# A bidirectional mLSTM and delta-rule encoder block on one core: one store of the inverses per half of the rows, another model behind the instruction order, and weight splits 60 places higher

## The chip, the cores and the metric

The kernel runs on one core of a Trainium2 chip. A core has five engines with a queue each: TensorE (PE, matrix products), VectorE (DVE), ScalarE (ACT), GpSimd (POOL) and SyncE (SP). Each takes its own instructions strictly in the order in which they stand in its queue, and the engines wait for each other through semaphores. Transfers are issued from the queues of SP, ACT and POOL. The metric is the device time of one execution, in microseconds; several executions are timed, and their median is given.

## The reference

One layer of an encoder for 256 tokens of width 2048, in float32. Cut to what matters here:

```python
mod = silu(c) @ W_ada + b_ada                 # six vectors: shift, scale, gate, twice
h = rms_norm(x) * (1 + scale_m) + shift_m
proj = h @ w_in                               # q,k,v,gates of mLSTM | q,k,v,z of GDN | merge gates
h_a = bidirectional(mlstm_chunkwise, ...)     # 4 heads of 256 x 512
o_b = bidirectional(gated_delta_chunkwise, ...)   # 16 heads of 128 x 128
x = x + gate_m * ((g_a * (h_a @ w_branch_a) + g_b * (o_b @ w_branch_b)) @ w_out)
hf = rms_norm(x) * (1 + scale_f) + shift_f
gt, up = split(hf @ w_gate_up)
x = x + gate_f * ((silu(gt) * up) @ w_down)
return rms_norm(x)
```

The delta rule (GDN) inverts a unit lower triangular matrix for each head and direction:

```python
a_mat = eye + beta * (k @ k.T) * decay_strict
t_mat = triangular_solve(a_mat, eye, lower=True, unit_diagonal=True)
u = t_mat @ (beta * v);  w = t_mat @ (beta * exp(g) * k)
```

## The kernel before

**Weights in two parts.** Every large product is run with weights and activations split in a high part (a cast to the fast float32 format) and a low part (the rest). A weight block of 1 MB is loaded to a buffer `raw` from SP's queue; ACT casts half of it to `wh` and DVE subtracts to get `wl` (128 x 1024 each); then PE multiplies high by high, high by low and low by high. `fjob` (from line 148) does so for a block of 128 output columns, products 256 wide; `tjob` (from line 169) for 512 columns, products 512 wide, two accumulators. Splits are lines 157 and 158 in `fjob`, 182 and 183 in `halves` of `tjob`. `raw`, `wh` and `wl` have three buffers each. A job is a generator; each step yields after half a block.

**Stages.** (1) The two adaLN vectors that the first norm needs are summed by DVE while the first 16 column blocks are multiplied. (2) Gates, convolutions and phase 1 of the first four delta-rule heads. (3) For each of four groups of four heads: `gdn_invert`, `gdn_blocks` and two passes of `gdn_phase2` (two heads each, some nine steps), while the next heads' projections (`b_job`, `fjob`) and the list `fills` (projections of z, of mLSTM and of the merge gates) give PE other work; the remaining adaLN sums run in the background on DVE, through the same `raw` buffers. (4) mLSTM beside the branch projections, then the output projection. (5) The feed-forward part: gate and up in 11 column groups, then down, and the final norm.

**The inverses.** Phase 1 of head h (from line 537) cuts the 32 x 32 diagonal blocks of its matrices, for two directions and two halves of the tokens, and moves them through DRAM (`inst_d`) so that each of the 16 blocks of a head is one partition of the tile `uu` (64 partitions, 32 x 32 each, for the four heads of a group): line 607, head `hl_` of the group to partitions 16 `hl_` to 16 `hl_` + 15. `gdn_invert` (from line 619) inverts all 64 blocks at once by back substitution on DVE, 30 pairs of instructions pinned in order. Rows 16 to 31 are final when i is 16, rows 0 to 15 at the end, and each half is stored by `store` (line 627): one transfer for each of the four heads, on POOL's queue, because `inv_d` holds the heads innermost. `gdn_blocks` (from line 650) loads the inverses from `inv_d` with four transfers, also POOL's, to a tile `cg`, transposes it on DVE (line 656), mixes it to `R` (lines 660 and 661) and copies it to `X` and `UL`. Phase 2 begins with products by `R` (line 689).

**What sets the order.** The program is traced in the order of the Python code, and each instruction gets its place in the trace as its priority. A scheduler then runs a model of the machine: whenever an engine of the model is free, it takes, of the instructions whose inputs and buffers are ready in the model, the one with the lowest place. What comes out is a fixed list for each engine. An instruction passed through `order` is pinned behind the one traced before it on its engine. So the list depends on how long the model thinks that instructions and transfers take; on the chip nothing is reordered any more, and an instruction that is not ready holds up all that stand behind it in its queue.

Of the kernel before, what the change touches and what calls it, by code (L numbers as in the profile page):

```python
# [9 lines left out]
F32 = mybir.dt.float32  # L10
F32R = mybir.dt.float32r
AF = mybir.ActivationFunctionType
ALU = mybir.AluOpType
# [8 lines left out]
NH_B, DK_B = 16, 128  # L22
# [2 lines left out]
KD = 11  # L25
GRP = 4
N0 = 4 + 3 * GRP


PK_ADAB = 0  # L30
# [22 lines left out]
def hybrid_block(ctx: ExitStack, tc: tile.TileContext, xr, nfr, crow, pk_d, cst_d, ada2, ada4, win0, winb, wint, wba, wbb, wo, wgu, wd, out, dbg=None):  # L53
    nc = tc.nc
    V, S, G, PE = nc.vector, nc.scalar, nc.gpsimd, nc.tensor
# [29 lines left out]
    def order(ins, yes=True):  # L85

        return tc.keep_in_program_order(ins) if yes else ins
# [60 lines left out]
    def fjob(name, src, done):  # L148

        ps = acc_ps.tile([P, 512], F32, tag="acc", name=f"acc_{name}")  # L150
        o = ps[:, :T]
        raw = st.tile([P, KB, P], F32, tag="raw", bufs=3, name=f"raw_{name}")
        nc.sync.dma_start(raw, src)
        for k0 in range(0, KB, 8):
            wh = st.tile([P, 8, P], F32R, tag="wh", bufs=3, name=f"wh_{name}_{k0}")
            wl = st.tile([P, 8, P], F32R, tag="wl", bufs=3, name=f"wl_{name}_{k0}")
            S.activation(wh, raw[:, k0 : k0 + 8], AF.Copy)  # L157
            V.tensor_tensor(wl, raw[:, k0 : k0 + 8], wh.bitcast(F32), ALU.subtract)  # L158
            for k in range(8):
                for i, x in enumerate((hh, hl)):  # L160
                    PE.matmul(o, wh[:, k], both(x, k0 + k).rearrange("p a b -> p b a"), start=k0 + k + i == 0, stop=False)  # L161
            for k in range(8):
                PE.matmul(o, wl[:, k], both(hh, k0 + k).rearrange("p a b -> p b a"), start=False, stop=k0 + k == KB - 1)
            if k0:
                pump()
                done(o.rearrange("p (b a) -> p a b", a=2))
            yield True

    def tjob(name, chunks, xh, xl, done, early=0, by_token=None, steps=1):

        raws = {}

        def halves(u, k0):
            if u not in raws:
                raws[u] = st.tile([P, 4, 512], F32, tag="raw", bufs=3, name=f"raw_{name}_{u}")
                nc.sync.dma_start(raws[u], chunks[u])
            wh = st.tile([P, 2, 512], F32R, tag="wh", bufs=3, name=f"wh_{name}_{u}_{k0}")  # L180
            wl = st.tile([P, 2, 512], F32R, tag="wl", bufs=3, name=f"wl_{name}_{u}_{k0}")
            order(S.activation(wh, raws[u][:, k0 : k0 + 2], AF.Copy), early)  # L182
            order(V.tensor_tensor(wl, raws[u][:, k0 : k0 + 2], wh.bitcast(F32), ALU.subtract), early)  # L183
            return wh, wl

        todo = [(u, k0) for u in range(len(chunks)) for k0 in (0, 2)]
        made = []
        for i, q in enumerate(todo[:early]):
            made.append(halves(*q))
            if steps > 1 or i == early - 1:  # L190
                yield True
        ps = [acc_ps.tile([P, 512], F32, tag="acc", name=f"acc_{name}_{t}") for t in range(2)]
        last = 4 * len(chunks) - 1
        if by_token:
            todo = todo[:-2]
        for n, (u, k0) in enumerate(todo):
            wh, wl = made.pop(0) if made else halves(u, k0)
            kt = [(4 * u + k0 + k, k, t) for k in range(2) for t in range(2)]
            for kk, k, t in kt:
                order(PE.matmul(ps[t], tok(xh, kk, t), turns(wh[:, k]), start=kk == 0, stop=False), early and steps > 1)  # L200
                PE.matmul(ps[t], tok(xl, kk, t), turns(wh[:, k]), start=False, stop=False)  # L201
            for kk, k, t in kt:
                PE.matmul(ps[t], tok(xh, kk, t), turns(wl[:, k]), start=False, stop=kk == last)  # L203
            if k0:
                pump()
                if u == len(chunks) - 1:
                    done(ps)
            yield True
            if early and steps > 1:
                if n + early < len(todo):  # L210
                    made.append(halves(*todo[n + early]))
                yield True
        if by_token:
            w = [halves(len(chunks) - 1, k0) for k0 in (0, 2)]
            by_token()
            for t in range(2):
                for k in range(4):
                    kk = last - 3 + k
                    wh = turns(w[k // 2][0][:, k % 2])
                    PE.matmul(ps[t], tok(xh, kk, t), wh, start=False, stop=False)  # L220
                    PE.matmul(ps[t], tok(xl, kk, t), wh, start=False, stop=False)
                for k in range(4):
                    kk = last - 3 + k
                    PE.matmul(ps[t], tok(xh, kk, t), turns(w[k // 2][1][:, k % 2]), start=False, stop=kk == last)
                done(t, ps[t])
                yield True
# [29 lines left out]
    mb_d = [tc.dram_tile([P, 2, 512], F32, name=f"mb_d{g}") for g in range(4)]  # L256
    ob_d = [tc.dram_tile([4, P, T], F32, name=f"ob_d{g}") for g in range(4)]
    inst_d = [tc.dram_tile([64, 32, 32], F32, name=f"inst_d{g}") for g in range(NH_B // GRP)]
    inv_d = [tc.dram_tile([32, 4, 16, 32], F32, name=f"inv_d{g}") for g in range(NH_B // GRP)]

    hh, hl = (bigA.tile([P, KB // 2, 2, 2, P], F32R, tag="b16", name=n) for n in ("hh", "hl"))

# [179 lines left out]
    with ExitStack() as s0:  # L442
        w0 = pool(s0, "w0")

        x = w0.tile([P, KB, T], F32, name="x")
        ss = w0.tile([P, 2], F32, name="ssx")
        rows = w0.tile([P, T], F32, name="rows")
# [13 lines left out]
        def loads(b):  # L461
            ra = [w0.tile([P, D + 2], F32, tag="ra", bufs=5, name=f"ra{b}_{i}") for i in range(2)]
            raw = st.tile([P, N0, P], F32, tag="raw", bufs=3, name=f"raw0_{b}")
            for i in range(2):
# [13 lines left out]
        ra, raw = loads(0)  # L478
# [18 lines left out]
        for b in range(KB):  # L497
            if b:
                ra, raw = loads(b)
# [35 lines left out]
    uus = {}  # L535

    def gdn_phase1(h):
# [61 lines left out]
        g, hl_ = divmod(h, GRP)  # L599
        if g not in uus:  # L600
            uus[g] = bk.tile([64, 32, 32], F32, tag="uu", bufs=1, name=f"uu{g}")
        inst = inst_d[g][16 * hl_ : 16 * hl_ + 16]
        for b in range(4):
            G.dma_start(
                inst[4 * b : 4 * b + 4].rearrange("x j i -> j x i"), mi[32 * b : 32 * b + 32, :, 32 * b : 32 * b + 32]
            )
        G.dma_start(uus[g][16 * hl_ : 16 * hl_ + 16], inst)

        cc = ccs[h % NB]
        for b in range(4):  # L610
# [8 lines left out]
    def gdn_invert(g):  # L619

        uu = uus.pop(g)
        tmp = bk.tile([64, 256], F32, tag="utmp", bufs=1, name=f"utmp{g}")
        inv = inv_d[g].rearrange("j b (x h) i -> h (b x) j i", h=GRP)

        def store(rows):
            for e in range(GRP):
                G.dma_start(inv[e, :, rows], uu[16 * e : 16 * e + 16, rows])

        yield
        order(V.memset(uu.rearrange("p j i -> p (j i)")[:, ::33], 1.0))  # L630
        size = 0
        for i in range(30, 0, -1):
            w = 31 - i
            t3 = tmp[:, 0 : i * w].rearrange("p (j c) -> p j c", j=i)
            order(V.tensor_tensor(
                t3,
                uu[:, 0:i, i : i + 1].broadcast_to([64, i, w]),
                uu[:, i : i + 1, i + 1 :].broadcast_to([64, i, w]),
                ALU.mult,
            ))  # L640
            order(V.tensor_tensor(uu[:, 0:i, i + 1 :], uu[:, 0:i, i + 1 :], t3, ALU.add))
            if i == 16:
                store(slice(16, 32))
            size += i * w + 125
            if size > 720:
                size = 0
                yield
        store(slice(0, 16))

    def gdn_blocks(g):  # L650

        cg = bk.tile([P, 2, 512], F32, tag="uu", bufs=1, name=f"cg{g}")
        for b in range(4):
            G.dma_start(cg[32 * b : 32 * b + 32, 0], inv_d[g][:, b].rearrange("j x i -> j (x i)"))
        yield
        order(V.transpose(cg[:, 1], cg[:, 0]))
        F_, Bt, Ft, B_ = (cg[:, i // 2, (i % 2) * 256 : (i % 2 + 1) * 256].rearrange("p (m c) -> p m c", m=8) for i in range(4))

        def mix(dst, a, ca, b, cb):
            order(V.tensor_scalar(dst, b, cb, None, ALU.mult))  # L660
            order(V.scalar_tensor_tensor(dst, a, ca, dst, ALU.mult, ALU.add))

        mix(R[:, 0], Ft, even, Bt, odd)
        mix(R[:, 1], B_, even, F_, odd)
        yield
        for i, ab in enumerate(((Ft, Bt), (B_, F_))):
            for b in range(4):
                r = slice(32 * b, 32 * b + 32)
                order(S.activation(X[r, i, :, b % 2], ab[b // 2][r], AF.Copy))
            yield  # L670
        for i, a in enumerate((F_, B_)):
            for b in range(4):
                r = slice(32 * b, 32 * b + 32)
                order(S.activation(UL[r, i, :, r], a[r], AF.Copy))
            yield
# [535 lines left out]
    for j in range(FB // 4):  # L1211
# [4 lines left out]
        for e2 in range(2):  # L1216
            px = gps(f"pxf{j}_{e2}")
            for e in range(2):
                f = 2 * e2 + e
                for t in range(2):  # L1220
                    PE.transpose(px[:, e * T + t * P : e * T + (t + 1) * P], sg[:, t, f * P : (f + 1) * P], ident)
            b = 4 * j + 2 * e2
# [143 lines left out]
```

## Time and profile before

| | |
|---|---|
| median of 3 runs | 2038.97 us (2037.25 to 2042.45) |
| the profiled execution | 2036.88 us, its span 2035.0 us |
| TensorE busy | 1956.7 us, 96% |
| VectorE, ScalarE, GpSimd busy | 1394.1, 1050.0 and 106.4 us |
| mean granted TensorE clock | 0.987 |
| DMA | 485.64 MB, 239 GB/s over the span |

The profile is one execution. Rows of groups give busy time, the mean duration in ns, the idle time of the engine ahead of the instruction and what ended it. PEld is TensorE's loading of weights, which overlaps its products. The granted clock is the share of full speed that TensorE was given. Times within the span count from its start. A wait is idle time of an engine, put down to what ended it.

### The profile page before, as it was taken

Reading aid. Unit: us, or ns where it says so; the run is one execution under the profiler, and the core shown is the slowest. Engines: PE = TensorE matmul, PEld = TensorE weight load, DVE = VectorE, ACT = ScalarE, POOL = GpSimd, SP = SyncE. Lnnn points to the kernel's source line nnn. Section 1 sums busy time; section 2 is a strip of 40 time slices with the busy share of each in tenths; the row PEclk is TensorE's granted clock in tenths of the full one; section 3 lists DMA queues with packets and bytes.
Section 4 is the critical chain, followed back from the end, with each engine's and each line's share of the span. In section 5 each row is a group of like instructions: output and inputs, shape, how many; then the busy total and the mean of one; then the engine's idle time right before and its main releaser. Section 6 shows DMA issues by size and latency. Waiting matters only on the chain.

```text
span 2035.0 us, 27065 instructions
## 1 busy us (share of the span) xinstructions
PE 1956.7 (96%) x10374; PEld 1706.4 (84%) x10374; DVE 1394.1 (69%) x2059; ACT 1050.0 (52%) x1582; POOL 106.4 (5%) x205
## 2 busy tenths in 40 slices
PE   8999999999999899999899999999999999999997
PEld 6777879988888788988878788778888888888886
DVE  5778777777889588855677679866666665555554
ACT  3147547755775577565444444554444444444443
POOL 0002210010101010100200000000000000000000
PEclk9999999999999899999999999999999999999999
DMA  9986664556766465766987669656767666566563
GB/s 399 420 325 222 178 215 153 190 171 220 241 230 197 178 211 212 243 238 240 360 297 264 212 245 390 256 186 249 252 244 262 235 246 212 204 206 204 199 200 142
DMA packets 78962, 485.64 MB, mean 239 GB/s; under 512 B 10585, under 2 KB 15969, under 8 KB 24433
## 3 DMA queue, kind: packets, MB, share of 16 engines
q1 hardware_dynamic: 63360, 450.95, 61.2%
q0 software_dynamic: 8160, 17.88, 3.8%
q10 hardware_dynamic: 7314, 15.10, 2.0%
q8 instruction: 81, 1.33, 0.3%
q14 instruction: 47, 0.39, 0.1%
HBM read 467.07 MB, written 16.82 MB: 238 GB/s over the span
## 4 chain that ended last, share of the span: by engine, by line
PE 70%; DMA 11%; DVE 9%; ACT 6%; issue 2%; POOL 1%; ACTq 0%; SPq 0%; DVEq 0%; POOLq 0%
PE acc_up L200 4%; PE acc_up L203 4%; PE acc_up L201 4%; PE acc_d L201 4%; PE acc_d L200 4%; PE acc_d L203 4%; PE acc_gt L201 4%; PE acc_gt L200 4%; PE acc_gt L203 4%; PE acc_b L161 3%; DMA ra<-ada 3%; DMA ada<-ada 2%; PE acc_o L203 2%; PE acc_o L200 2%; PE acc_o L201 2%
## 5 line engine op out<-in xcount | busy, mean ns | idle before, releaser
L183 DVE TENSOR_TENSOR wl_d<-raw_d,wh_d 128x1024 fp32r<-128x1024 f32 x88 | 107.5, 1225 | 105.4 <-ACT wh_d L182 103.1
L183 DVE TENSOR_TENSOR wl_up<-raw_up,wh_up 128x1024 fp32r<-128x1024 f32 x88 | 107.6, 1225 | 100.4 <-ACT wh_up L182 100.4
L126 DVE SCALAR_TENSOR_TENSOR ada<-ada,crow 128x2048 f32<-128x2048 f32 x64 | 146.6, 2290 | 24.1 <-DMA ada<-ada 24.0
L182 ACT ACTIVATE wh_d<-raw_d 128x1024 fp32r<-128x1024 f32 x88 | 92.9, 1056 | 124.5 <-PE acc_d L201 114.3
L183 DVE TENSOR_TENSOR wl_gt<-raw_gt,wh_gt 128x1024 fp32r<-128x1024 f32 x88 | 107.7, 1224 | 69.9 <-ACT wh_gt L182 68.4
L182 ACT ACTIVATE wh_up<-raw_up 128x1024 fp32r<-128x1024 f32 x88 | 92.9, 1057 | 120.9 <-PE acc_up L201 71.6
L161 PE MATMUL acc_b<-hh,wh_b 128*128 128x256 f32 x576 | 142.0, 288 | 9.6 <-ACT wh_b L157 8.0
L182 ACT ACTIVATE wh_gt<-raw_gt 128x1024 fp32r<-128x1024 f32 x88 | 92.9, 1055 | 108.9 <-PE acc_gt L201 61.3
L161 PE MATMUL acc_b<-hl,wh_b 128*128 128x256 f32 x576 | 139.6, 284 | 0.0
L201 PE MATMUL acc_gt<-wh_gt,hfl 128*128 128x512 f32 x352 | 136.9, 389 | 0.0
L200 PE MATMUL acc_gt<-wh_gt,hfh 128*128 128x512 f32 x352 | 135.6, 385 | 0.0
L200 PE MATMUL acc_up<-wh_up,hfh 128*128 128x512 f32 x352 | 133.4, 379 | 0.0
L201 PE MATMUL acc_up<-wh_up,hfl 128*128 128x512 f32 x352 | 133.4, 379 | 0.0
L200 PE MATMUL acc_d<-wh_d,ffh 128*128 128x512 f32 x344 | 130.8, 380 | 0.0
L201 PE MATMUL acc_d<-wh_d,ffl 128*128 128x512 f32 x344 | 130.5, 379 | 0.0
L161 PEld LDWEIGHTS acc_b<-hh,wh_b 128*128 128x128 f32 x576 | 114.6, 199 | 10.2 <-ACT wh_b L157 8.5
L511 PE MATMUL first<-x,raw 128*128 128x256 f32 x512 | 114.5, 382 | 6.6 <-ACT x L504 6.6
L511 PEld LDWEIGHTS first<-x,raw 128*128 128x128 f32 x512 | 96.0, 190 | 25.1 <-ACT x L504 12.6
L161 PEld LDWEIGHTS acc_b<-hl,wh_b 128*128 128x128 f32 x576 | 114.8, 199 | 0.0
L300 DVE SCALAR_TENSOR_TENSOR cv<-pad,pk,cv 128x256 f32<-128x256 f32 x192 | 90.8, 481 | 20.2 <-ACT cv L298 18.2
L158 DVE TENSOR_TENSOR wl_b<-raw_b,wh_b 128x1024 fp32r<-128x1024 f32 x72 | 86.9, 1220 | 23.7 <-ACT wh_b L157 20.6
L182 ACT ACTIVATE wh_o<-raw_o 128x1024 fp32r<-128x1024 f32 x64 | 67.4, 1056 | 60.1 <-PE acc_o L201 27.2
(369 smaller groups left out, 5016.4 us busy)
## 6 DMA issues: line engine op xcount, KB each, us to landing
ada<-ada SPq DMA_DIRECT2D x64, 1024.0 KB, 5.2
raw_gt<-wgu SPq DMA_DIRECT2D x44, 1024.0 KB, 5.0
raw_up<-wgu SPq DMA_DIRECT2D x44, 1024.0 KB, 4.9
raw_d<-wd SPq DMA_DIRECT2D x44, 1024.0 KB, 4.9
raw_b<-winb SPq DMA_DIRECT2D x36, 1024.0 KB, 5.1
ra<-ada SPq DMA_DIRECT2D x32, 1025.0 KB, 15.7
raw<-win SPq DMA_DIRECT2D x16, 1024.0 KB, 14.5
raw_z<-wint SPq DMA_DIRECT2D x16, 1024.0 KB, 5.1
```

The costliest lines, as they stand in the source:

```text
L126: V.scalar_tensor_tensor(raw, raw, 1.0, row_c[:, :D], ALU.mult, ALU.mult, accum_out=mod[:, c0 + b : c0 + b + 1])
L158: V.tensor_tensor(wl, raw[:, k0 : k0 + 8], wh.bitcast(F32), ALU.subtract)
L161: PE.matmul(o, wh[:, k], both(x, k0 + k).rearrange("p a b -> p b a"), start=k0 + k + i == 0, stop=False)
L182: order(S.activation(wh, raws[u][:, k0 : k0 + 2], AF.Copy), early)
L183: order(V.tensor_tensor(wl, raws[u][:, k0 : k0 + 2], wh.bitcast(F32), ALU.subtract), early)
L200: order(PE.matmul(ps[t], tok(xh, kk, t), turns(wh[:, k]), start=kk == 0, stop=False), early and steps > 1)
L201: PE.matmul(ps[t], tok(xl, kk, t), turns(wh[:, k]), start=False, stop=False)
L203: PE.matmul(ps[t], tok(xh, kk, t), turns(wl[:, k]), start=False, stop=kk == last)
L300: V.scalar_tensor_tensor(cv, pd[:, i : i + T], w[i], cv, ALU.mult, ALU.add)
L511: PE.matmul(first[o], raw[:, o], x[:, b], start=b == 0 and o % 2 == 0, stop=b == KB - 1 and o % 2 == 1)
```

## The change

Three things are changed together.

1. `uu` is laid out with the heads innermost: head `hl_` of a group goes to partitions `hl_`, `hl_` + 4 and so on, and `inv_d` becomes a tensor of 32 x 64 x 32 in the same order of partitions. A half of the rows is then stored with one transfer in place of four. The loads of `cg` read the same places.
2. The scheduler's model of the machine is another: the timeline simulator in place of the default one. This holds for the whole kernel.
3. The splits of weights in `fjob` and in `tjob` get a priority 60 places lower in number, that is, earlier, than where they are traced. Jobs that start with splits pinned ahead (`early`) are left as they were.

The program traces the same instructions for all engines but POOL; ACT's loads of function tables are put in by the compiler after the order is set.

```diff
+AHEAD = 60
@@ fjob
-            S.activation(wh, raw[:, k0 : k0 + 8], AF.Copy)
-            V.tensor_tensor(wl, raw[:, k0 : k0 + 8], wh.bitcast(F32), ALU.subtract)
+            with tc.high_priority(AHEAD):
+                S.activation(wh, raw[:, k0 : k0 + 8], AF.Copy)
+                V.tensor_tensor(wl, raw[:, k0 : k0 + 8], wh.bitcast(F32), ALU.subtract)
@@ tjob, halves
-            order(S.activation(wh, raws[u][:, k0 : k0 + 2], AF.Copy), early)
-            order(V.tensor_tensor(wl, raws[u][:, k0 : k0 + 2], wh.bitcast(F32), ALU.subtract), early)
+            with tc.high_priority(0 if early else AHEAD):
+                order(S.activation(wh, raws[u][:, k0 : k0 + 2], AF.Copy), early)
+                order(V.tensor_tensor(wl, raws[u][:, k0 : k0 + 2], wh.bitcast(F32), ALU.subtract), early)
@@ hybrid_block
-    inv_d = [tc.dram_tile([32, 4, 16, 32], F32, name=f"inv_d{g}") for g in range(NH_B // GRP)]
+    inv_d = [tc.dram_tile([32, 64, 32], F32, name=f"inv_d{g}") for g in range(NH_B // GRP)]
@@ gdn_phase1
-        G.dma_start(uus[g][16 * hl_ : 16 * hl_ + 16], inst)
+        G.dma_start(uus[g][hl_::GRP], inst)
@@ gdn_invert
-        inv = inv_d[g].rearrange("j b (x h) i -> h (b x) j i", h=GRP)
         def store(rows):
-            for e in range(GRP):
-                G.dma_start(inv[e, :, rows], uu[16 * e : 16 * e + 16, rows])
+            G.dma_start(inv_d[g][rows].rearrange("j p i -> p j i"), uu[:, rows])
@@ gdn_blocks
-            G.dma_start(cg[32 * b : 32 * b + 32, 0], inv_d[g][:, b].rearrange("j x i -> j (x i)"))
+            G.dma_start(cg[32 * b : 32 * b + 32, 0], inv_d[g][:, 16 * b : 16 * b + 16].rearrange("j m i -> j (m i)"))
@@ kernel
-    with tile.TileContext(nc) as tc:
+    with tile.TileContext(nc, schedule_with_timeline_sim=True) as tc:
```

## The prediction

> **What bounds the kernel now.** I read the page's busy times first, then stretches of the span, then TensorE's waits, and last the stretch after each inversion.
>
> ```profile
> span 2035.0 us, 27065 instructions
> PE 1956.7 (96%) x10374; PEld 1706.4 (84%) x10374; DVE 1394.1 (69%) x2059; ACT 1050.0 (52%) x1582; POOL 106.4 (5%) x205
> ```
>
> TensorE (PE) is the bound: busy 96%, so no order of the same work can take off more than its 78 us of idle time, plus what a reduced clock costs. The stretches say where that is. After the times come PE's busy time and instructions, the weight loads', VectorE's (DVE), ScalarE's (ACT), GpSimd's (POOL), the granted clock, the DMA share and GB/s.
>
> ```profile
> 0.00:137.00 137.00, 127.36 (x550) 104.37 (x551) 93.21 (x111) 31.11 (x59) 2.41 (x12) 1.00 0.98 402
> 137.00:300.00 163.00, 154.49 (x698) 129.84 (x696) 130.18 (x269) 99.66 (x154) 30.08 (x55) 0.98 0.64 211
> 300.00:520.00 220.00, 209.70 (x1452) 193.01 (x1452) 164.37 (x318) 151.52 (x281) 20.46 (x40) 0.98 0.56 184
> 520.00:700.00 180.00, 169.31 (x1150) 155.47 (x1150) 140.41 (x282) 117.55 (x211) 20.66 (x40) 0.96 0.63 209
> 700.00:900.00 200.00, 190.31 (x1275) 173.51 (x1275) 157.02 (x297) 130.21 (x239) 18.07 (x34) 0.99 0.65 221
> 900.00:1000.00 100.00, 92.98 (x576) 84.26 (x575) 57.09 (x78) 53.61 (x91) 10.56 (x17) 0.98 0.77 282
> 1000.00:1300.00 300.00, 296.17 (x1349) 246.23 (x1348) 230.43 (x284) 135.77 (x175) 4.13 (x8) 0.99 0.79 292
> 1300.00:1350.00 50.00, 41.56 (x185) 33.42 (x184) 30.82 (x48) 30.57 (x53) 0.00 (x0) 0.93 0.41 148
> 1350.00:1800.00 450.00, 450.00 (x2116) 390.15 (x2115) 271.83 (x262) 200.88 (x215) 0.00 (x0) 1.00 0.67 236
> 1800.00:2035.00 235.00, 224.79 (x1039) 196.17 (x1038) 118.79 (x114) 99.16 (x110) 0.00 (x0) 0.99 0.55 188
> ```
>
> The first 137 us are bound by the transfers (DMA share 0.98) and pinned in program order; from 1350 to 1800 PE has no idle time at all. So the change can gain only between 137 and 1350 us. There PE is idle for 8.5+10.3+10.7+9.7+7.0+3.8+8.4 = 58.5 us, and the clock column loses (one minus the clock, times the length) 3.3+4.4+7.2+2.0+2.0+3.0+3.5 = 25.4 us. What PE waits for (total, times, longest):
>
> ```profile
> PE acc_b L161 <- ACT wh_b L157: 8.0, 3, 3.7
> PE acc_o L203 <- DVE wl_o L183: 5.5, 2, 3.5
> PE acc_z L200 <- ACT wh_z L182: 4.8, 3, 2.8
> PE p L689 <- DVE R L661: 4.6, 2, 2.6
> PE vps L555 <- ACT vf L301: 3.2, 5, 1.4
> PE acc_mb L203 <- DVE wl_mb L183: 2.6, 3, 1.4
> PE p L698 <- DVE pt L690: 2.3, 2, 1.5
> PE acc_v L203 <- DVE wl_v L183: 2.0, 1, 2.0
> PE acc_b L163 <- DVE wl_b L158: 1.6, 1, 1.6
> PE acc_z L203 <- DVE wl_z L183: 1.6, 2, 1.2
> PE acc_ma L203 <- DVE wl_ma L183: 0.8, 1, 0.8
> ```
>
> The eight rows of wh and wl are waits for splits of weights: 8.0+5.5+4.8+2.6+2.0+1.6+1.6+0.8 = 26.9 us. Three rows (p, vps, p) are waits for the delta rule's own steps: 10.1 us in 9 waits.
>
> **Part one: the stores of the inverses.** The timeline of POOL and DVE at the end of the first inversion, and the sum of DVE's waits for the load that follows:
>
> ```profile
> 284.24 2.23 POOL L627 DMA_DIRECT2D inv_d<-uu  x4 [15.45 <-DVE uu L641]
> 291.24 1.99 POOL L654 DMA_DIRECT2D cg<-inv_d  x4 [4.77 <-DMA inv_d<-uu]
> 299.95 0.71 DVE L656 STREAM_TRANSPOSE cg<-cg 128x512 f32<-128x512 f32 x1 [8.62 <-DMA cg<-inv_d]
> 300.81 1.22 DVE L183 TENSOR_TENSOR wl_o<-raw_o,wh_o 128x1024 fp32r<-128x1024 f32 x1
> DVE cg L656 <- DMA cg<-inv_d: 28.4, 4, 8.6
> ```
>
> Four stores take 2.23 us of POOL, land 4.8 us later, four loads follow, and DVE stands at the transposing instruction for 8.6 us. Behind it in DVE's queue stands wl_o, a split, and PE's longest wait for wl_o (3.5 us) is here. All four groups together hold DVE for 28.4 us.
>
> The change issues one store in place of four for each half. What one such issue costs the trace doesn't show. The nearest rows:
>
> ```profile
> L627 POOL DMA_DIRECT2D inv_d<-uu x32 | 17.9, 566 | 144.9 <-DVE uu L641 125.5 <-DVE utmp L635 19.4
> L911 POOL DMA_DIRECT2D bc<-mal_d x8 | 4.3, 546 | 9.6 <-DMA mkq<-kq_d 3.3 <-DMA raw_yb<-wbb 2.4 <-DMA vt<-v_d 2.2
> L895 POOL DMA_DIRECT2D o<-ob_d x4 | 3.1, 770 | 103.3 <-ACT wh_a L157 100.1 <-DMA sgo<-o_d 2.7 <-DMA bc<-mal_d 0.5
> ```
>
> By the code bc moves 128 contiguous runs and o moves 512: (770-546)/384 = 0.58 ns a run. The new store has 64 x 16 = 1024 runs of 128 bytes: 546 + 896 x 0.58 = 1.07 us, an estimate, against 2.23: 1.2 us less in each group. At the other end the price grows with the runs, 4 x 566 ns, and nothing is gained. The bytes and runs in flight are the same, so I leave the landing as it is. 4 x 1.2 = 4.8 us if PE gets all of it; R is awaited twice and wl_o once directly, so I take **-4 us** (ends -4.8 and 0). The 24 issues fewer on POOL are worth nothing more, as POOL is 5% busy. The first half's store isn't on the path: 15 further pairs of the inversion's steps follow it. The loads of uu (now to every fourth partition) and of cg are as many and as large as before. No wait is added: the one store waits for what the first of four waited for.
>
> **Part two: splits 60 places higher.** No instruction is added. A split is a cast on ACT and a subtraction on DVE:
>
> ```profile
> L157 ACT ACTIVATE wh_b<-raw_b 128x1024 fp32r<-128x1024 f32 x72 | 74.8, 1055 | 29.5 <-DMA raw_b<-winb 14.2 <-PE acc_b L161 13.2 <-PE acc_mb L201 1.5
> L158 DVE TENSOR_TENSOR wl_b<-raw_b,wh_b 128x1024 fp32r<-128x1024 f32 x72 | 86.9, 1220 | 23.7 <-ACT wh_b L157 20.6 <-PE acc_b L163 2.5
> ACT wh_d L182 <- PE acc_d L201: 114.3, 75, 2.0
> ```
>
> In the last matrix of the feed-forward part the splits already run as early as their buffers allow: ACT waits 114.3 us for PE to free one, and PE never waits. There the higher place is free of effect, hidden under a full PE. Between 137 and 1350 us a split that was ready but stood behind a convolution, a scan or an eviction now goes first. The pot is 26.9 - 3.5 (the wait behind the transpose, a matter of the stores and the order) = 23.4 us. Ends: all of it, or nothing, since a split that waits for its raw load or its buffer gains nothing from a place (14.2 and 13.2 us of ACT's idle time ahead of wh_b are of these kinds, about half to each). I take half: **-12 us**.
>
> What is overtaken is late by one split, 1.06 us on ACT or 1.22 on DVE. Had each of the 9 waits for the delta rule one more split ahead of it, that is 9 x 1.22 = 11 us; the other end is 0, since PE has other groups' products to run meanwhile. I take **+6**. Raw loads on SP's queue aren't raised; a buffer freed sooner only lets the next be issued sooner. An adaLN sum (2.3 us on DVE) that is overtaken keeps its raw buffer longer, and the next weight load behind it on SP's queue waits; it is in the +6.
>
> **The clock.** Two stretches of 1 us after the 2.0 us wait for wl_v:
>
> ```profile
> 215.00:216.00 1.00, 0.00 (x0) 0.00 (x0) 1.00 (x3) 0.70 (x2) 0.00 (x0) 1.00 1.01 394
> 219.00:220.00 1.00, 1.00 (x4) 0.91 (x5) 0.34 (x4) 0.56 (x3) 0.00 (x0) 0.50 1.00 66
> ```
>
> PE stands still at 215, and then works at half clock. So a wait costs more than its length, and only a wait that goes altogether, or nearly, gives the clock back. Of the 58.5 us idle the two parts take 16, 27%; 27% of the clock's 25.4 would be 7; as many waits will be shortened and not removed I take **-3** (ends -7 and 0).
>
> The Trainium skill, "TensorE: Matmul & The Clock Gate", Part 1, puts the drop to half rate after an idle window of about 3.4 us; here 2.0 us was enough. By the page's figure just the 3.5 and the 3.7 us waits would count, and cutting both a little would give back about 2 x 3.4 us of clock, a sum of -19 where mine is -15 (an estimate by that page); the trace disagrees with it, so mine stays.
>
> **Part three: the timeline model.** It sets the order of every instruction that isn't pinned, on all engines. No row tells which of the two models is nearer to the chip. The four stalls at the transposes (28.4 us) are places where the present model had the load land too early, and with it the splits behind; a model that had it land later would put those splits first and give PE most of the 3.5+4.6 us, and clock, back, some -10. At the other end the new order makes waits of its own: half as many again as the 58.5 us now, +29. One such price can be seen, ACT's function tables:
>
> ```profile
> L301 ACT ACT_TABLE_LOAD x21 | 26.9, 1283 | 0.4
> L787 ACT ACT_TABLE_LOAD x14 | 18.0, 1283 | 0.2
> ```
>
> A table is loaded where two neighbours in ACT's list need different ones, so another order has more or fewer of these, 1.28 us of ACT each; ten more would be 13 us of an engine that is 65% busy there, beside PE's work, and lie within these ends. For the whole part I take **-2**, near nought, as the waits left are those of a list that fits its model but not the chip, and a second list will have such waits too.
>
> **Sum**: -4 - 12 + 6 - 3 - 2 = -15 us on the profiled execution's 2036.88 us (its span 2035.0 and 1.9 around it): 2021.9. The runs' median, 2038.97, stands 2.1 above that execution, so I forecast **2024 us**.
>
> **Rivals.** *Nothing to tell*: splits wait for buffers and loads, not for places, and the new order only moves waits about. For it: the 114.3 us row; against it: 23.4 us of waits for splits in stretches where DVE is busy 75 to 80% of the time. Then only the stores count, -4: 2035.
>
> *Slower*: the delta rule is starved. Between 300 and 900 us DVE is busy 461.8 of 600 us. Phase 2 is eight passes of some nine dependent steps, 72, in which PE, DVE and ACT take turns. With splits always first, a step meets one ahead of it on the chip (1.22 us) that the model thought done. If one step in three shows on PE, 24 x 1.22 = 29 us; against it stand the -4 and -12: +13, 2052. It decides from about 13 exposed steps on, where 13 x 1.22 eats the 16 gained. For it: PE already waits on p, vps and p in 9 places. Against it: PE's list has the projections to fill with.
>
> *Large gain*: the timeline model also puts the four transposes where the load really lands. All of part two's 23, the stores' 4.8, the clock's 7 and the order's 5 come, less 3 for what is overtaken: -37, 2002. Against it: it needs each term at its good end.
>
> **How the numbers follow.** Forecast (gain of 6 to 25 us, 2014 to 2033) 0.44; large gain 0.15; no change that can be told 0.18; slower 0.23. What can be told from no change here is 0.3%, 6 us. So faster 0.59, same 0.18, slower 0.23. The range reaches to both outer rivals, 2000 to 2054: it holds the stores at nothing, the order between -20 and +15, and leaves out a tenth on either side.
>
> **What would show it.** Stores: 8 issues of inv_d, each 1 to 1.1 us, and DVE's waits at the transpose below 24 us in all. Splits: the eight rows of wh and wl at about half of 26.9 us. Overtaken work: p, vps and p at 16 us or less. Clock: above 0.98 from 300 to 700 us. From 1350 to 1800 us PE stays without idle time; if it doesn't, a cover that I counted on is gone. The forecast is wrong if waits for splits don't fall, or if waits on the delta rule's lines grow by more than they fall.

## The result, and the profile after

The changed kernel takes 2025.3 us, median of 4 runs (2022.47 to 2027.92), beside a median of 2038.11 for the kernel before on the same chip: a ratio of 0.9933 (95% interval 0.9911 to 0.9955), 13 us or 0.7% faster. The forecast was 2024. Its profiled execution took 2027.92 us, the longest of the four.

First the busy times of the changed kernel's profile, then the stretches of its span (columns as in the prediction).

```profile
span 2026.1 us, 27066 instructions
PE 1948.1 (96%) x10374; PEld 1707.8 (84%) x10374; DVE 1386.5 (68%) x2059; ACT 1037.3 (51%) x1571; POOL 95.0 (5%) x181
```

```profile
137.00:300.00 163.00, 154.76 (x714) 131.06 (x714) 133.11 (x271) 104.29 (x158) 25.26 (x45) 0.98 0.66 209
300.00:520.00 220.00, 213.61 (x1513) 198.91 (x1512) 166.44 (x328) 151.71 (x285) 19.64 (x38) 0.99 0.61 198
520.00:700.00 180.00, 171.80 (x1177) 158.76 (x1176) 143.78 (x285) 113.21 (x210) 17.73 (x34) 0.97 0.64 211
700.00:900.00 200.00, 194.45 (x1252) 176.72 (x1251) 153.16 (x291) 127.72 (x233) 15.29 (x28) 1.00 0.66 232
900.00:1000.00 100.00, 85.39 (x538) 77.61 (x537) 53.02 (x70) 49.69 (x88) 7.37 (x12) 0.92 0.73 256
1000.00:1300.00 300.00, 294.49 (x1344) 245.55 (x1342) 229.21 (x291) 130.19 (x172) 7.32 (x12) 0.99 0.78 290
1300.00:1350.00 50.00, 41.58 (x183) 34.50 (x184) 30.52 (x46) 32.18 (x53) 0.00 (x0) 0.90 0.38 128
1350.00:1800.00 450.00, 450.00 (x2126) 393.52 (x2124) 270.04 (x263) 201.78 (x214) 0.00 (x0) 1.00 0.66 238
```

From 300 to 900 PE's idle time falls from 30.7 to 20.1 us; from 900 to 1000 it rises from 7.0 to 14.6 and the clock falls from 0.98 to 0.92. From 137 to 1350 the idle time is 56.9 us (58.5 before), and the clock's loss, worked out as in the prediction, 26.9 us (25.4 before). So the two accounts that the prediction kept are as large as before, and the span is still 8.9 us shorter: PE's busy time is 8.6 us less for the same 10374 products.

**An account that holds the gain.** "Busy" covers products that start late and those at half clock. So I took the starts of all PE products, and counted as lost what the interval to the next start has above the usual one for that shape (the 40th percentile over the executions below; intervals shorter than usual count against it). This takes waits, half clock and short gaps together, for the profiled executions, in us. Later work also stands at slightly other times, so neighbouring stretches are to be read together.

| kernel | 300 to 900 | 900 to 1000 | elsewhere | whole span |
|---|---|---|---|---|
| before | 47.9 | 9.5 | 54.6 | 112.0 |
| changed | 32.8 | 17.5 | 51.5 | 101.8 |
| changed, run again | 31.7 | 16.4 | 48.3 | 96.4 |

The gain of 15 us lies in the three stretches of the delta rule; 8 of them are given back where the branch projection starts. The second row and the third are one kernel (`after_again` below): two executions differ by 5 us, and differences of that size between kernels tell nothing.

**What stood at the transpose is gone.** First inversion in the changed kernel, timeline of POOL, then of DVE, then DVE's waits for `cg` in sum.

```profile
298.98 0.83 POOL L628 DMA_DIRECT2D inv_d<-uu  x1 [20.99 <-DVE uu L642]
304.56 2.00 POOL L655 DMA_DIRECT2D cg<-inv_d  x4 [4.74 <-DMA inv_d<-uu]
```

```profile
299.08 1.22 DVE L160 TENSOR_TENSOR wl_b<-raw_b,wh_b 128x1024 fp32r<-128x1024 f32 x1 [0.40 <-ACT wh_b L159]
301.73 1.23 DVE L160 TENSOR_TENSOR wl_b<-raw_b,wh_b 128x1024 fp32r<-128x1024 f32 x1 [1.42 <-ACT wh_b L159]
304.59 1.23 DVE L160 TENSOR_TENSOR wl_b<-raw_b,wh_b 128x1024 fp32r<-128x1024 f32 x1 [1.64 <-ACT wh_b L159]
305.73 1.52 DVE L303 SCALAR_TENSOR_TENSOR cv<-pad,pk,cv 128x256 f32<-128x256 f32 x3
307.17 1.22 DVE L160 TENSOR_TENSOR wl_b<-raw_b,wh_b 128x1024 fp32r<-128x1024 f32 x1
308.31 0.48 DVE L303 SCALAR_TENSOR_TENSOR cv<-pad,pk,cv 128x256 f32<-128x256 f32 x1
309.33 0.71 DVE L657 STREAM_TRANSPOSE cg<-cg 128x512 f32<-128x512 f32 x1 [0.55 <-DMA cg<-inv_d]
```

```profile
DVE cg L657 <- DMA cg<-inv_d: 2.2, 2, 1.7
```

The store is one transfer, issued in 0.83 us. Between the inversion's end and the transpose DVE's list now holds four splits and four convolution steps, where it held five splits. DVE waits 0.55 us at the transpose where it waited 8.6, and in all four groups 2.2 us where it was 28.4.

The list is not the whole reason. By the timelines of the four groups, the stretch from the inversion's end to the transpose is 55.6 us in all, 60.2 before. DVE works in 30.7 us of it, 23.7 before, and waits for other things, mostly casts, in 22.7, 8.1 before. In the first group the load is also there sooner: the transpose starts 10.4 us after the store, 15.7 before.

**The new wait.** PE's waits for splits and for the delta rule in the changed kernel (`pb`, `px` and `pa` are steps of phase 2 too), and above them the longest:

```profile
PE acc_yb L203 <- ACT obh L900: 13.2, 1, 13.2
PE acc_z L206 <- DVE wl_z L186: 7.2, 1, 7.2
PE acc_b L163 <- ACT wh_b L159: 6.4, 7, 1.3
PE vps L558 <- ACT vf L304: 3.3, 2, 3.1
PE p L724 <- DVE pt L713: 2.6, 3, 2.0
PE acc_yb L206 <- DVE wl_yb L186: 2.2, 1, 2.2
PE pb L748 <- ACT z L740: 2.0, 2, 1.0
PE px L773 <- DVE on L793: 1.8, 2, 1.7
PE acc_mb L203 <- ACT wh_mb L185: 1.4, 1, 1.4
PE px L773 <- ACT obt L775: 1.4, 1, 1.4
PE p L690 <- DVE R L662: 1.3, 1, 1.3
PE acc_o L206 <- DVE wl_o L186: 0.8, 2, 0.6
PE acc_v L206 <- DVE wl_v L186: 0.7, 1, 0.7
PE pa L736 <- ACT UL L725: 0.7, 1, 0.7
PE p L699 <- DVE pt L691: 0.4, 2, 0.2
PE acc_z L203 <- ACT wh_z L185: 0.4, 1, 0.4
```

Splits: 7.2+6.4+2.2+1.4+0.8+0.7+0.4 = 19.1 us (26.9 before). The three kinds of wait for the delta rule that the prediction summed: 5.0 (10.1 before). But with all its rows the delta rule's waits are as large as before: 5.0+2.6+2.0+1.8+1.4+0.7 = 13.5 us, and before 10.1 with `pc` 1.1, `pb` 1.1, `px` 1.0 and another row of `p` 0.3 = 13.6. And there are 13.2 us of a kind that was not there: the branch projection `acc_yb` needs the delta rule's outputs, loaded to `o` and cast to `obh`. The timeline and two stretches of the changed kernel:

```profile
982.98 1.57 POOL L896 DMA_DIRECT2D o<-ob_d  x2 [124.46 <-ACT wh_yb L185]
994.38 1.06 ACT L900 ACTIVATE obh<-o 128x1024 fp32r<-128x1024 f32 x1 [9.12 <-DMA o<-ob_d]
```

```profile
982.00:995.49 13.49, 0.29 (x3) 0.00 (x1) 1.25 (x2) 4.29 (x5) 5.75 (x9) 0.59 1.00 352
995.49:1002.00 6.51, 6.47 (x15) 4.69 (x16) 5.06 (x5) 2.12 (x2) 3.08 (x5) 0.53 1.02 383
```

The loads are issued as PE runs dry, and the cast that waits for them starts 9.8 us after their issue; the DMA share is 1.00 in that stretch. Then PE works at a clock of 0.53 for 6.5 us. In the kernel before, `acc_yb` started at 1012.1 us without such a wait. PE's list held other products until then, and PE's one long wait there was this:

```profile
PE psc L924 <- DMA mkq<-kq_d: 5.3, 1, 5.3
```

It is gone in the changed kernel, so the new wait costs less than its length: 8 us by the table.

### The profile page after: what moved, and what is told of

It is laid out like the page before. It is cut to its first block, busy times and chain, and to the rows that moved or that the text cites. A ratio compares the mean times of both kernels' runs of the same rounds, so it can differ in the third digit from the quotient of the medians.

```text
span 2026.1 us, 27066 instructions
## 1 busy us (share of the span) xinstructions
PE 1948.1 (96%) x10374; PEld 1707.8 (84%) x10374; DVE 1386.5 (68%) x2059; ACT 1037.3 (51%) x1571; POOL 95.0 (5%) x181
## 4 chain that ended last, share of the span: by engine, by line
PE 74%; DMA 9%; DVE 8%; ACT 6%; issue 3%; POOL 0%; ACTq 0%; SPq 0%; DVEq 0%; POOLq 0%
PE acc_up L206 4%; PE acc_up L203 4%; PE acc_up L204 4%; PE acc_d L206 4%; PE acc_d L204 4%; PE acc_d L203 4%; PE acc_gt L206 4%; PE acc_gt L204 4%; PE acc_gt L203 4%; DMA ra<-ada 3%; PE acc_b L163 2%; PE acc_a L163 2%; PE acc_o L206 2%; PE acc_o L204 2%; PE acc_o L203 2%
## 5 line engine op out<-in xcount | busy, mean ns | idle before, releaser
L159 ACT ACTIVATE wh_b<-raw_b 128x1024 fp32r<-128x1024 f32 x72 | 75.3, 1057 | 56.9 <-DMA raw_b<-winb 30.5
## 6 DMA issues: line engine op xcount, KB each, us to landing
ra<-ada SPq DMA_DIRECT2D x32, 1025.0 KB, 15.7
```

## The experiments

All ratios are to the kernel before on the same chip, in the same job, with a 95% interval. PE's, DVE's and the other engines' instruction lists are fixed in a kernel, so two kernels' lists can be compared line by line.

**Each part alone.**

`store_only`: part one alone, without places and with the old model.

```diff
-        G.dma_start(uus[g][16 * hl_ : 16 * hl_ + 16], inst)
+        G.dma_start(uus[g][hl_::GRP], inst)
-            for e in range(GRP):
-                G.dma_start(inv[e, :, rows], uu[16 * e : 16 * e + 16, rows])
+            G.dma_start(inv_d[g][rows].rearrange("j p i -> p j i"), uu[:, rows])
```

> The new layout and the one store per half, with the model and the places of before. PE's list is that of before; DVE's and ACT's differ in a few lines. If the shorter chain reaches PE as forecast: 2034 us, 4 less than before. If DVE's stall at the transpose is covered by other groups' products: 2038, no change. In both, DVE's wait at the transpose falls by 1.2 to 1.4 us in each group, from 28.4 to about 23 us.

Measured: 2024.62 us, 0.9949 (0.9929 to 0.9969), 10.9 us faster. PE's list is the same as before, line for line, so no product was moved in it. POOL's wait for the store, of the kernel before and of this one, and this one's waits at the transpose:

```profile
POOL cg L654 <- DMA inv_d<-uu: 22.0, 4, 7.3
```

```profile
283.65 0.83 POOL L628 DMA_DIRECT2D inv_d<-uu  x1 [16.84 <-DVE uu L642]
287.50 2.01 POOL L655 DMA_DIRECT2D cg<-inv_d  x4 [3.02 <-DMA inv_d<-uu]
POOL cg L655 <- DMA inv_d<-uu: 13.9, 4, 4.5
DVE cg L657 <- DMA cg<-inv_d: 17.4, 4, 6.3
```

In the first group it is 3.85 us from the start of the store to the loads here, and 7.00 before (291.24 less 284.24). The issue is 1.4 us shorter, and the rest is the landing: in all four groups 13.9 us of waits in place of 22.0, 2.0 a group. DVE's waits at the transpose fall by 11.0 us, about what the kernel gained; by the count of the table above, PE loses 39.3 us from 300 to 900 in this profile in place of 47.9, so 8.6 us of the gain stand there.

The sooner landing is not a property of the one store. With the old model POOL waits 13.9 to 16.9 us where the store is one transfer (`store_only`, `no_model`, `best_old`, `best_turn`) and 18.5 to 22.0 where it is four. With the timeline model it is the other way round: 15.3 us with four stores (`model_only`), 18.6 with one (the changed kernel). Why is open.

`place_only`: part two alone.

```diff
+AHEAD = 60
@@ fjob
+            with tc.high_priority(AHEAD):
@@ tjob, halves
+            with tc.high_priority(0 if early else AHEAD):
```

> Splits 60 places higher, with the stores and the model of before. Theory A (the forecast: the places carry the gain): -12 + 6 - 3, about 2029 us, and the waits of PE for wh and wl fall from 26.9 to about 14 us. Theory B (the model carries it): 2036 to 2040, and those waits stay above 20 us.

Measured: 2026.9 us, 0.9952 (0.9936 to 0.9968), 8.6 us by the medians. The longest of PE's waits:

```profile
PE p L693 <- DVE R L665: 13.8, 3, 8.4
```

The waits for splits fall from 26.9 to 10.1 us, and those for R rise from 4.6 to 13.8. On the side of the splits, with the old model, places do what the prediction said of them. On the other side they do something else. The longest wait for R, 8.4 us, comes right behind DVE's stall at the transpose, and ends at 860.19 us; no split stands between that transpose and the R that PE waits for:

```profile
858.58 0.71 DVE L660 STREAM_TRANSPOSE cg<-cg 128x512 f32<-128x512 f32 x1 [8.05 <-DMA cg<-inv_d]
```

So it is the old stall, which stands in PE's way here; DVE's waits at the transposes are still 22.2 us.

`place20`: part two alone, with 20 places.

```diff
-AHEAD = 60
+AHEAD = 20
```

> Splits 20 places higher in place of 60; stores and model of before. If overtaking is what gains, 20 places let fewer splits go first: 2028 to 2034 us, PE's waits for wh and wl between 10 and 27 us. If any other list of the same work is as good as 60 places: 2024 to 2029 us, whatever these waits are.

Measured: 2032.32 us, 0.9978 (0.996 to 0.9996). Waits for splits 22.8 us, at the transposes 25.2: 20 places overtake little, and give little. Its interval overlaps that of `place_only`.

`model_only`: part three alone.

```diff
-    with tile.TileContext(nc) as tc:
+    with tile.TileContext(nc, schedule_with_timeline_sim=True) as tc:
```

> The timeline model with the stores and the places of before. Theory A: 2036 us, 2 less than before. Theory B: 2024 to 2029 us, nearly all of the gain; DVE's wait at the transpose falls from 28.4 us to a few, because the transposes stand later in its list.

Measured: 2027.08 us, 0.9959 (0.9946 to 0.9973), 8.5 us. Compared place by place in the traces, some 3100 of PE's 10374 products and over 1100 of DVE's 2059 instructions are others than before.

```profile
PE acc_yb L203 <- ACT obh L903: 11.5, 1, 11.5
DVE cg L660 <- DMA cg<-inv_d: 3.4, 2, 2.8
```

Both signs of the changed kernel are here without its other parts: the stall at the transposes is all but gone, and PE stands before the branch projection. The splits' waits (17.9 us) are the changed kernel's too.

**The changed kernel without one part.**

`no_place`: the places are taken back.

```diff
-AHEAD = 60
+AHEAD = 0
```

> The changed kernel without the higher places. Its lists differ from the changed kernel's in 5 lines of PE's and 4 of DVE's. Theory A: 2034 us. Theory B: 2025 us, as the changed kernel, with its 13 us wait for obh.

Measured: 2024.95 us, 0.9949 (0.9935 to 0.9963). Only 5 lines of PE's list and 4 of DVE's differ from the changed kernel. Under the timeline model the 60 places move next to nothing, and the forecast's largest term has nothing to stand on. As `no_place` is the model with the stores, beside `model_only` it also shows what one store adds there: 0.9949 against 0.9959, intervals overlapping, waits at the transposes 3.6 us against 3.4. Nothing can be told.

`no_model`: the model is taken back; stores and places stay.

```diff
-    with tile.TileContext(nc, schedule_with_timeline_sim=True) as tc:
+    with tile.TileContext(nc) as tc:
```

> Stores and places changed, the model of before. Each of the two alone gave a ratio of 0.995. Theory C (each takes away waits of its own): the gains add, about 2017 us, below the changed kernel. Theory D (all parts take away the same stall behind the inversions, once): 2023 to 2027 us, as each alone. Under C PE's waits for wh and wl stay at or below 10 us and the 13.8 us wait for R of the places alone falls by half.

Measured: 2028.59 us, 0.9951 (0.9933 to 0.9968).

```profile
PE acc_o L206 <- DVE wl_o L186: 7.9, 3, 6.2
PE p L690 <- DVE R L662: 7.2, 2, 5.9
DVE cg L657 <- DMA cg<-inv_d: 30.3, 4, 10.5
300.94 0.71 DVE L657 STREAM_TRANSPOSE cg<-cg 128x512 f32<-128x512 f32 x1 [10.47 <-DMA cg<-inv_d]
```

Two parts that gave 10.9 and 8.6 us alone give 10 together. The stores do arrive early (4.02 to 5.80 us from store to loads), and over the four groups it is 47.2 us from the inversion's end to the transpose, 60.2 before. The stall is still as large as in the kernel before, because DVE has less to do until then. Its list holds 14 splits (16.5 us of work) between the four inversions and their transposes, where it holds 20 (23.7 us) in the kernel before, 18 in `store_only`, and 20 with two other instructions in `place_only`. So the shorter chain is not used: the order asks for the transpose sooner. By the count of lost time PE loses 43.6 us from 300 to 900, more than with either part alone (39.3 and 37.4). Why the scheduler placed the transposes so early is open.

`after_again`: the changed kernel once more, with no edit, to see its scatter.

> The changed kernel again, beside these: 2025 us and a ratio of 0.991 to 0.996 again, PE's wait for obh of 11 to 13 us.

Measured: 2026.82 us, 0.9949 (0.9932 to 0.9965).

**Is it the place of the transposes?**

`late_turn`: the kernel before, old model and old stores, with four more pieces of other work traced ahead of the transpose, so that it comes later in DVE's list.

```diff
         next(blocks)
-        fill(8)
+        fill(12)
         next(blocks)
```

> The kernel before, with the transposes of the inverses traced after 12 half jobs of the list of fills in place of 8; stores, model and places as before. If the stall of DVE at the transposes (28.4 us in four groups, splits queued behind) is what all parts relieve: DVE's wait there falls below 8 us and the time to 2024 to 2029 us. If the stall is covered: 2034 to 2038 us. If a later start of phase 2 costs more: above 2040.

Measured: 2033.31 us, 0.9972 (0.9959 to 0.9985); the 2024 to 2029 us that were expected if the stall decides did not come. DVE no longer waits for `cg` at all. The stretches of this kernel, and its new wait:

```profile
300.00:520.00 220.00, 216.71 (x1481) 199.18 (x1480) 160.71 (x312) 148.60 (x272) 20.61 (x40) 0.99 0.57 188
...
900.00:1000.00 100.00, 84.55 (x560) 77.74 (x558) 56.08 (x75) 57.24 (x113) 3.05 (x5) 0.95 0.71 246
```

```profile
PE acc_yb L200 <- ACT obh L899: 11.8, 1, 11.8
```

One number in the program makes most of what the model gained (lost time from 300 to 900: 35.7 us, 47.9 before) and what it gave back (16.9 us from 900 to 1000, 9.5 before). The two are one trade: work put ahead of the transposes is work that is no longer there at the end. Counted in PE's list, the products between the delta rule's last step and the first of `acc_yb` are worth 35.4 us at their usual intervals in the kernel before and in `store_only`, 5.8 in the changed kernel, and none in `late_turn` (the 16 products `psc`, which wait for loads of their own, left out).

**Can the loss be had back?**

`last_fewer`: the changed kernel, with fewer pieces of other work between the last group's steps.

```diff
-    last = (0, 1, 2, 1, 2, 2, 1, 1, 3, 0)
+    last = (0, 1, 1, 1, 1, 1, 1, 1, 2, 0)
```

> The changed kernel, with 9 in place of 13 half jobs drawn between the steps of each of the last group's two passes, so that more is left to run behind them. If PE's wait of 13 us for obh is there because the list of fills is used up before the last pass ends: the wait falls below 5 us, half a clock spell goes with it, 2012 to 2018 us. If the scheduler fills PE with the same jobs anyway: the same order and 2023 to 2027 us.

Measured: 2024.19 us, 0.9928 (0.991 to 0.9946), the wait for `obh` 11.7 us. The cover, as these products may be called, is 6.7 us in place of 5.8: traced later, they still stand ahead of the last steps in PE's list. That cure fell.

`z_free`: the changed kernel, with the later splits of jobs that begin with pinned ones set free, and 60 places higher like the others. It is aimed at the 7.2 us wait for `wl_z`.

```diff
-        def halves(u, k0):
+        def halves(u, k0, early=early):
...
-            wh, wl = made.pop(0) if made else halves(u, k0)
+            wh, wl = made.pop(0) if made else halves(u, k0, 0)
```

> The changed kernel, with only the first three half jobs of the first z projection pinned; its later splits are free and 60 places higher. If the 7.2 us wait for wl_z near 150 us comes from splits pinned behind the convolutions on DVE: it falls below 2 us, the half clock after it goes, 2014 to 2020 us. If DVE is simply full there, the convolutions come later, the first heads with them, and the time stays at 2023 to 2027 us.

Measured: 2022.32 us, 0.9918 (0.9901 to 0.9934), the lowest median of all. The wait for `wl_z` is gone, splits cost 10.4 us in all, and this comes in its place, with `obh` as before:

```profile
PE ptr L437 <- DVE tr L426: 5.4, 1, 5.4
PE acc_yb L203 <- ACT obh L900: 12.3, 1, 12.3
```

Its interval overlaps the changed kernel's, so it isn't shown to be faster, and the 2014 to 2020 us that were expected if only the pinned splits were to blame did not come.

`best_old`: the stores with the edit of `z_free`, old model, no places; as edits of `z_free`:

```diff
-AHEAD = 60
+AHEAD = 0
-    with tile.TileContext(nc, schedule_with_timeline_sim=True) as tc:
+    with tile.TileContext(nc) as tc:
```

`best_turn`: the same with a later turn.

```diff
-        fill(8)
+        fill(10)
```

> The stores alone (model and places of before), with the later splits of the first z projection not pinned. The stores alone gave 0.995. Theory E (the stores shorten DVE's stall without using up the products that cover the start of the next stage): 300 to 900 us as in the run with the stores alone, no wait of PE for obh, 2018 to 2025 us; at or below the changed kernel. If pinning z's splits was worth nothing with this model: 2025. If the gain of the stores alone was chance: 2030 and above.

> The same, with the transposes traced after 10 half jobs in place of 8. In PE's list 15 us of products are left between the last pass and the branch projection, 35 us without the later transposes, 6 us in the changed kernel. Theory E: DVE's wait at the transposes falls below 8 us, but the cover is thin, PE waits some us for obh or psc, and the time is that of the run without it, within 5 us. If the stall alone decides: 2010 to 2016 us.

Measured: 2025.53 us, 0.9946 (0.993 to 0.9962), and 2030.17 us, 0.9956 (0.994 to 0.9972). The later turn cuts the waits at the transposes from 20.9 to 6.8 us and splits from 22.5 to 10.2, and nothing is won: lost time from 900 to 1000 rises from 6.1 to 15.2 us, as the cover falls to 14.9. No arrangement of the old model tried here is shown to beat the changed kernel. Loading `o` earlier, which would go at the wait for `obh` itself, wasn't tried.

## Why the prediction was right, and where it was not

The time is right (2024 forecast, 2025.3 measured) and so is the direction. The sum that led there is not: none of its five terms came as priced in the changed kernel, and that the errors cancelled is luck.

**Splits higher, -12: this step fails for the changed kernel.** "A split that was ready but stood behind a convolution, a scan or an eviction now goes first" is true with the old model: in `place_only` the waits for splits fall by 16.8 us. In the changed kernel it is worth nothing that can be told (`no_place`). I priced each part against the old order, though part three replaces that order. The waits for splits still fell, to 71% of the prediction's eight rows (a ninth, `wh_a` with 0.3 us, was left out), where about half was foreseen; `model_only` has 17.9 us of them, so it is the model's doing.

**Overtaken work, +6.** No run shows its size. In `place_only` the waits for R rise from 4.6 to 13.8 us, but most of that is the stall at the transpose and not a split ahead of R. In the changed kernel `p`, `vps` and `p` fell to 5.0, so "16 or less" held; but places move next to nothing there, and with the rows that the prediction left out the delta rule's waits are 13.5 us, 13.6 before.

**Stores, -4, ends -4.8 and 0: the mechanism holds, the size was off.** One store is issued in 0.85 us, not 1.07. "I leave the landing as it is" failed with the old model: in `store_only` POOL waits 2.0 us less a group, and the chain from the store to the loads is 2.8 to 4.3 us shorter in each group, not 1.2. Alone the part gave 10.9 us, outside my ends even at its weaker bound (6.3). In the changed kernel it adds nothing that can be told: the wait it shortens is no longer there, and the chain itself is only 0.6 us a group shorter than in `model_only` (21.9 and 24.2 us in all from store to loads).

On the price of the issue the Trainium skill, "DMA: Bandwidth & Descriptors", "Anatomy of one DMA — SWDGE (gpsimd) path", has it that many descriptors can be emitted before their cost shows. The traces agree in part: 546 ns for 128 runs, 770 for 512 and 851 for 1024. The cost does show, but the line is flatter than my straight one.

**Timeline model, -2, ends -20 and +29: mis-sized, and its two halves were both there.** Alone it measured -8.5. The half I had priced at "some -10" is the 15 us from 300 to 900. `late_turn` shows that a later place of the transposes alone is worth 12 of them; it does not show that the model's gain is all of this kind. The other half, "waits of its own", is the 13.2 us before `acc_yb` with the half clock after it; by the table it costs 8 us. I had looked for covers only in the stretches where the stalls were. Most of the 35.4 us of products that shielded the branch projection were used up elsewhere, and this should have been named as the price of any later transpose.

**The clock, -3.** It didn't come: 26.9 us by the windows, 25.4 before. From 300 to 520 the clock is 0.99, but from 520 to 700 it is 0.97, where above 0.98 was foreseen, and from 900 to 1000 it fell. The sum of -19 that the prediction sets beside its own takes 3.4 us at half clock as 3.4 us lost; at half clock half of the time is lost, which makes that sum -15 too.

**From 1350 to 1800** PE has no idle time, as foreseen.

**The rivals.** The delta rule isn't starved: its waits stayed as they were. "Nothing to tell" and the large gain lie outside the interval of 0.9911 to 0.9955 (2020 to 2029 us). The large gain's condition, transposes where the load lands, was met; what it lacked was everything else, since the parts don't add: alone 10.9, 8.6 and 8.5 us, the two pairs that were run 10 and 11, all three 13 and, run again, 11. That both remove the one stall at the transposes explains the stores with the model (waits there 3.6 and 3.4 us). The stores with places don't add for another reason: that order reaches the transposes with less work done, and the stall is back (30.3 us).

## What to carry to other kernels

Where one of several edits replaces the order of all instructions, price the others against the new order, not the old. Work that is moved ahead to cover one wait is taken from somewhere: find what it covered there, and what that stage waits for first. And when idle time and clock don't account for a gain, count the intervals between the bound engine's starts.

## What the runs showed that was not expected

A single store of 1024 runs of 128 bytes from 64 partitions is issued in 0.85 us; four stores with the same bytes took 2.23. How long POOL then waits in the four groups hangs on the order around the stores as much as on their number: 13.9 to 18.9 us for one store, 15.3 to 22.0 for four.

After the 13.2 us wait PE works at about half clock for some 6 us: 6.5 us at a mean of 0.53, a loss of 3 us. The Trainium skill, "TensorE: Matmul & The Clock Gate", Part 1, gives about 3.4 us of sustained work until the full rate is back, and counts them in windows that run freely. Here it took nearly twice that; a window that had begun before PE did could account for it.

The order also set how often ACT loads a function table, against the direction that the prediction had feared: ACT has 1571 instructions in place of 1582 and is 12.7 us less busy. At line 788 (787 before) the table loads fell from 14 to 5, though at line 567 (564 before) they rose from 9 to 12. What this gave to PE no run shows by itself.
